# A hybrid S5, attention and MoE layer on one core: the opening's modulation, normalisation and S5 operator in another order

## The chip, the core and the metric

One core of a Trainium2 chip runs the whole kernel. The metric is the device time of one execution in microseconds. Three runs of the kernel before gave 2739.33 to 2745.31 us, with a median of 2741.16 us.

## The reference: what is computed

A layer over 1024 latent tokens of width 1024 and 256 context tokens, all in float32. Cut to what the opening touches:

```python
mod = silu(c) @ w_mod + b_mod              # for the latent and for the context vector
h   = layer_norm(x, g, b)                  # latent rows and context rows
u   = h * (1 + scale1) + shift1            # modulate
p   = u @ w_in                             # S5 input, q, k, v, gates
y   = S5_bidir(gelu input from p)          # 32 groups of 16 channels, 64 states
mix = W_o(sig(g_s) * W_s(GLU(y)) + sig(g_a) * W_a(attention))
h   = LN(alpha * h + gate1 * mix)
h   = LN(alpha * h + gate2 * MoE(modulate(h, shift2, scale2)))
```

The S5 recurrence is computed in blocks of 8 tokens: for each of 32 groups the kernel builds an operator within a block and the operators into and out of the state, from lam, b, c and d.

## The kernel before

The work up to about 300 us is called the opening here. It is written as Python generators, and `weave` takes one step of each in turn; `limit(gen, n)` takes at most n steps. That sets the order in which each engine gets its instructions, and each engine runs its own list strictly in that order. SyncE (SP) issues nearly all DMAs, also in order.

The parts, with their lines in the profile:

- `s5_consts`: the constants of the S5 blocks on DVE, with two loads of s5p.
- `mod_cols` (L1798): shift1 and scale1 as columns. Eight loads of w_mod (1 MB each, L1814, two buffers) feed 32 matmuls (L1827) with the two condition vectors `cs` stationary (2 columns) and 512 columns of w_mod moving, which leaves a row of 2x512; the trace shows two passes for each float32 matmul. ACT copies the row to SBUF (`mr`, L1831) and 16 transposes (L1834) turn it into columns of the PSUM tile `mod`. DVE adds the bias (`mc`, L1836) and makes the scale A and the shift B (L1843 to L1846).
- `ln_rows` (L1849), three groups: context, latent tiles 0 to 3, latent tiles 4 to 7. DVE takes BN_STATS (L78), a chain of small operations for the reciprocal root (L61 to L72) and normalises (L1860); the normalised latent rows are stored (`xhat_d`, L1862).
- `ln_cols` (L1866), the same three groups: PE transposes (L1874), ACT applies A and B (`f`, L1876) and takes the high part (`ch` or `uh`, L42), DVE the low part (`cl` or `ul`, L43). They are the moving and stationary sides of all projections, in which each product is three matmuls (L51 to L53).
- `s5_build` (L2107): for each of eight quarters of the groups `out(q)` makes `ca` on POOL (L2133 to L2135; the last two on DVE), `within(q)` copies `zb` (L2143), stores `ca` (`wout_d`, L2144), runs the matmuls `pm` and `pc` (L2151, L2154), evicts them (`qs`, L2157 to L2159) and stores eight pieces (`m_d`, L2162). `into(q)` makes `ba` on DVE (`cmul`, L1974 to L1981), transposes it (L2174), copies it to the one buffer `wi` on ACT (L2175) and stores it (`win_d`, L2177).
- `s_in(0)`, `s_in(1)` (L269): the projections of both halves of the S5 input. PE runs 24 matmuls for each step, ACT evicts `r` (L285); at the end of a half PE transposes it to `U` (L290, L295) and DVE copies U (L292, L296).
- `s5_state` (L355): loads the stored operator back (`wi`, L361), 16 groups `yp` for each half (L367), and their evictions `XS` on ACT and DVE (L370 to L372).
- `mod_rows` (L674): the six other parts of w_mod as rows. DVE multiplies and adds them (`macc`, L699, started by L701), eight pieces for each of eight chunks, with PE and DVE ending a chunk (L687, L688).
- After them `kv_rows`, `q_rows`, `gates`, `state_powers` (L379) and the scan.

In the kernel before, `opening` puts `out`, `within` and `into` between the normalisation and the columns, so part of the operator is built before the first projection.

Of the kernel before, what the change touches and what calls it, by code (L numbers as in the profile page):

```python
# [8 lines left out]
F32 = mybir.dt.float32  # L9
# [1488 lines left out]
def weave(*jobs):  # L1498

    jobs = [j for j in jobs if j is not None]  # L1500
    while jobs:
        for j in jobs[:]:
            if next(j, jobs) is jobs:
                jobs.remove(j)
# [293 lines left out]
def mod_cols(tc, a, K, xp, tmp):  # L1798

    nc = tc.nc  # L1800
    cst = K.cst
    sg = xp.tile([128, 16], F32, name="sg")
    cs = cst.tile([128, 8, 2], F32, name="cs")
    nc.scalar.activation(out=sg, in_=K.cols[:, 0:16], func=ACTF.Sigmoid)
    nc.vector.tensor_tensor(cs.rearrange("p k j -> p j k"), K.cols[:, 0:16].rearrange("p (j k) -> p j k", j=2),
                            sg.rearrange("p (j k) -> p j k", j=2), ALU.mult)
    K.cs = cs
    ws = []

    def load(n):  # L1810
        if n < 8:
            j, k = n // 2, n % 2 * 4
            w = K.wp.tile([128, 4, 512], F32, tag="raw", name="raw")
            nc.sync.dma_start(out=w, in_=a["w_mod"][k * 128:(k + 4) * 128, j * 512:(j + 1) * 512].rearrange("(k p) n -> p k n", p=128))  # L1814
            ws.append(w)

    load(0)
    load(1)
    yield
    tps = K.s5ps.tile([128, 512], F32, tag="mod", name="mod")  # L1820
    for j in range(4):
        p = K.mm.tile([128, 512], F32, tag="mm", name="mm")
        for h in range(2):
            w = ws.pop(0)
            for i in range(4):
                k = h * 4 + i
                nc.tensor.matmul(p[0:2, :], lhsT=cs[:, k, :], rhs=w[:, i, :], start=k == 0, stop=k == KT - 1)  # L1827
            load(2 * j + h + 2)
            yield
        mr = tmp.tile([128, 512], F32, tag="f", name="mr")[0:2]  # L1830
        nc.scalar.activation(out=mr, in_=p[0:2, :], func=ACTF.Copy)  # L1831
        for i in range(4):
            n = j * 4 + i
            nc.tensor.transpose(tps[:, 2 * n:2 * n + 2], mr[:, i * 128:(i + 1) * 128], K.ident[0:2, 0:2])  # L1834
    mc = xp.tile([128, 16, 2], F32, name="mc")
    nc.vector.tensor_tensor(mc, tps[:, 0:32].rearrange("p (a b) -> p a b", b=2),  # L1836
                            K.cols[:, 32:48].unsqueeze(2).to_broadcast([128, 16, 2]), ALU.add)
    K.A = cst.tile([128, 8, 2], F32, name="A")
    K.B = cst.tile([128, 8, 2], F32, name="B")
    g = K.cols[:, 16:24].unsqueeze(2).to_broadcast([128, 8, 2])  # L1840
    b = K.cols[:, 24:32].unsqueeze(2).to_broadcast([128, 8, 2])
    s1 = xp.tile([128, 8, 2], F32, name="s1")
    nc.vector.tensor_scalar(s1, mc[:, 8:16, :], 1.0, None, ALU.add)  # L1843
    nc.vector.tensor_tensor(K.A, s1, g, ALU.mult)
    nc.vector.tensor_tensor(K.B, s1, b, ALU.mult)
    nc.vector.tensor_tensor(K.B, K.B, mc[:, 0:8, :], ALU.add)  # L1846


def ln_rows(tc, a, K, xs, src, t0, n):  # L1849

    nc = tc.nc
    mv = K.sm.tile([128, 4, 2], F32, tag="mv", name="mv")
    r = K.sm.tile([128, 4], F32, tag="lir", name="lir")
    for i in range(n):
        ln_stats(nc, K.sm, xs[src, t0 + i], mv[:, i, :], "li")
        yield
    rsqrt(nc, K.sm, r[:, 0:n], mv[:, 0:n, 1], n, "li%d" % n)
    for i in range(n):
        x = xs[src, t0 + i]
        nc.vector.tensor_scalar(x, x, mv[:, i, 0:1], r[:, i:i + 1], ALU.subtract, ALU.mult)  # L1860
        if src == "x":
            nc.sync.dma_start(out=K.xhat_d[(t0 + i) * 128:(t0 + i + 1) * 128, :], in_=x)  # L1862
        yield
# [26 lines left out]
def opening(tc, a, K, pool, ls, fs, cs):  # L1890
# [21 lines left out]
    loads = [("x", 0, K.wp, "wlo"), ("x", 2, K.wp, "whi"), ("x", 4, K.wp, "wlo"), ("x", 6, hp, "x")]  # L1912
    load("ctx", 0, K.wp, "whi")
    next(s5)
    rows = [ln_rows(tc, a, K, xs, *g) for g in GROUPS]
    cols = [ln_cols(tc, a, K, tmp, xs, *g) for g in GROUPS]
    next(mods)
    weave(limit(s5, 31))
    next(mods)
    load(*loads.pop(0))  # L1920
    weave(s5, rows[0])
    next(mods)
    load(*loads.pop(0))
    outs, ins = s5_build(tc, a, K, sb)
    weave(limit(mods, 2))
    for x in loads:
        load(*x)
    weave(limit(mods, 2))
    next(outs)
    weave(limit(mods, 1))  # L1930
    w0, w1 = (load_raw(tc, K, a["w_in"][:, c * 256:(c + 1) * 256]) for c in range(2))
    weave(rows[1])
    weave(mods)
    weave(cols[0], rows[2])
    next(outs)
    weave(cols[1], limit(ins, 4))
    next(outs)
    w0 = load_w(tc, K, None, raw=w0)
    nc.sync.dma_start(out=K.rope, in_=a["rope"].rearrange("p (t j d) -> p t j d", t=8, j=3))
    weave(cols[2], limit(ins, 8))  # L1940
    next(outs)
    ls.close()
    K.rin = pool(cs, "rin", 1, side="right")
    w1 = load_w(tc, K, None, raw=w1)
# [18 lines left out]
def limit(gen, n):  # L1963
    for _ in range(n):
        if next(gen, gen) is gen:
            return
        yield
# [293 lines left out]
```

## Time and profile before

| | |
|---|---|
| runs | 2739.33 to 2745.31 us, median 2741.16 us |
| profiled execution | 2747.31 us, span 2745.2 us |
| PE busy | 2513.9 us (92%) |
| DVE busy | 2175.9 us (79%) |
| ACT busy | 1465.1 us (53%) |
| POOL busy | 275.4 us (10%) |
| granted clock of the core | 0.948 mean |

Busy shares over the whole span hide the stage at issue: the opening is a tenth of the span. It is read by stretches: the busy time and the granted clock between two events, the order of the events on each engine, and for each idle stretch the instruction that ended it.

### The profile page before, as it was taken

How to read it: one execution, taken by the hardware profiler on the slowest of the kernel's cores; microseconds unless marked ns; L12 is line 12 of the kernel's file. 1: busy time of each engine (PE TensorE's matmuls, PEld its weight loads, DVE VectorE, ACT ScalarE, POOL GpSimd, SP SyncE). 2: the span in 40 equal slices, each digit the busy share in tenths (PEclk: the TensorE clock that was granted, in tenths of full speed). 3: DMA queues.
4: the chain of work that ended last, by engine and by line, in shares of the span. 5: the costliest groups of instructions: out<-in, count | busy, mean ns of one | idle time of the engine just before them, and what ended most of it. 6: DMA issues, size and time to landing. Idle time of an engine off the chain costs nothing.

```text
span 2745.2 us, 41252 instructions
## 1 busy us (share of the span) xinstructions
PE 2513.9 (92%) x14030; PEld 2115.1 (77%) x14030; DVE 2175.9 (79%) x4203; ACT 1465.1 (53%) x2368; POOL 275.4 (10%) x173
## 2 busy tenths in 40 slices
PE   6799999888989886899999999999999999999990
PEld 1598887777778774788888878888988887888770
DVE  9635797337787757787887987988899899989995
ACT  0622112657766412565655655666666666666661
POOL 3300000000000004011010110111011111101103
PEclk8799999999999876899999999999999999999995
DMA  7434623544686783797987987998998999899974
GB/s 245 165 121 146 212 85 119 179 153 160 222 308 246 288 289 116 229 292 221 287 275 231 309 277 235 312 300 254 290 303 274 286 312 303 278 293 306 315 269 146
DMA packets 400934, 662.55 MB, mean 241 GB/s; under 512 B 36976, under 2 KB 203760, under 8 KB 393616
## 3 DMA queue, kind: packets, MB, share of 16 engines
q1 hardware_dynamic: 388416, 615.83, 67.2%
q0 software_dynamic: 11872, 42.47, 6.7%
q8 instruction: 112, 1.84, 0.3%
q10 hardware_dynamic: 432, 1.57, 0.2%
q14 instruction: 102, 0.84, 0.1%
HBM read 570.63 MB, written 89.15 MB: 240 GB/s over the span
## 4 chain that ended last, share of the span: by engine, by line
PE 46%; DVE 6%; issue 4%; DMA 2%; ACT 1%; POOL 0%; POOLq 0%; SPq 0%; DVEq 0%; ACTq 0%
PE uw L1360 14%; PE uw L1361 7%; PE dn L1307 6%; PE dn L1308 6%; PE dn L1310 5%; DVE wl L1494 2%; PE tp L1278 2%; PE up L1307 2%; PE up L1310 2%; PE up L1308 2%; DMA acc_d<-y,wi 1%; DVE oh L1198 1%; PE sl L1214 1%; ACT wh L1492 1%; PE up L1321 1%
## 5 line engine op out<-in xcount | busy, mean ns | idle before, releaser
L1494 DVE TENSOR_TENSOR wl<-raw,wh 128x1024 fp32r<-128x1024 f32 x768 | 921.6, 1220 | 162.7 <-ACT wh L1492 161.6
L1492 ACT ACTIVATE wh<-raw 128x1024 fp32r<-128x1024 f32 x768 | 789.5, 1052 | 243.5 <-PE dn L1310 88.7
L1360 PE MATMUL uw<-x,wh 128*128 128x320 f32 (+5 forms) x1920 | 580.5, 366 | 0.2 <-issue 0.2
L1361 PE MATMUL uw<-x,wl 128*128 128x192 f32 (+4 forms) x1920 | 501.2, 261 | 0.0
L1360 PEld LDWEIGHTS uw<-x,wh 128*128 128x128 f32 x1920 | 364.4, 190 | 23.8 <-issue 0.3
L1361 PEld LDWEIGHTS uw<-x,wl 128*128 128x128 f32 x1920 | 369.3, 192 | 0.5
L1307 PE MATMUL dn<-wh,a 128*128 128x512 f32 (+4 forms) x752 | 298.6, 397 | 0.0
L1308 PE MATMUL dn<-wl,a 128*128 128x512 f32 (+4 forms) x752 | 293.5, 390 | 0.0
L1310 PE MATMUL dn<-wh,a 128*128 128x512 f32 (+3 forms) x608 | 238.5, 392 | 0.6 <-DVE a L1287 0.6
L1307 PE MATMUL up<-wh,x 128*128 128x512 f32 x544 | 221.8, 408 | 0.0
L1443 POOL DMA_INDIRECT acc_d<-y,wi x47 | 120.7, 2568 | 959.2 <-DVE y L1441 815.9
L1310 PE MATMUL up<-wh,x 128*128 128x512 f32 x544 | 213.0, 392 | 0.0
L1308 PE MATMUL up<-wl,x 128*128 128x512 f32 x544 | 212.3, 390 | 0.0
L1372 ACT ACTIVATE t<-uw,bias 128x160 f32<-128x160 f32 (+5 forms) x240 | 98.6, 419 | 134.7 <-PE uw L1361 134.0
L1307 PEld LDWEIGHTS dn<-wh,a 128*128 128x128 f32 (+4 forms) x752 | 135.7, 180 | 37.8 <-issue 4.1
L1308 PEld LDWEIGHTS dn<-wl,a 128*128 128x128 f32 (+4 forms) x752 | 135.8, 181 | 33.8
L1310 PEld LDWEIGHTS dn<-wh,a 128*128 128x128 f32 (+3 forms) x608 | 112.8, 186 | 28.4 <-DVE a L1287 2.7
L1307 PEld LDWEIGHTS up<-wh,x 128*128 128x128 f32 x544 | 102.3, 188 | 27.4 <-issue 8.4
L1310 PEld LDWEIGHTS up<-wh,x 128*128 128x128 f32 x544 | 102.1, 188 | 22.4
L1308 PEld LDWEIGHTS up<-wl,x 128*128 128x128 f32 x544 | 102.4, 188 | 18.8
L51 PE MATMUL mm<-whi,uh 128*128 128x256 f32 x320 | 108.2, 338 | 4.7 <-DVE r L307 4.7
L52 PE MATMUL mm<-wlo,uh 128*128 128x256 f32 x320 | 107.5, 336 | 0.0
(528 smaller groups left out, 4939.8 us busy)
## 6 DMA issues: line engine op xcount, KB each, us to landing
raw<-w_gate_up SPq DMA_DIRECT2D x512, 512.0 KB
raw<-w_down SPq DMA_DIRECT2D x256, 512.0 KB
mw<-w_mod SPq DMA_DIRECT2D x64, 256.0 KB
raw<-w_in SPq DMA_DIRECT2D x13, 1024.0 KB
whi<-wo SPq DMA_DIRECT2D x10, 1024.0 KB
wlo<-wo SPq DMA_DIRECT2D x10, 1024.0 KB
raw<-w_mod SPq DMA_DIRECT2D x8, 1024.0 KB
gate_d<-gs SPq DMA_DIRECT2D x16, 512.0 KB
```

The lines of the kernel that those rows point to most:

```text
L51: nc.tensor.matmul(out, lhsT=lsel(lh, k), rhs=rsel(rh, k), start=start and k == 0, stop=False)
L52: nc.tensor.matmul(out, lhsT=lsel(lh, k), rhs=rsel(rl, k), start=False, stop=False)
L1278: nc.tensor.transpose(p[:, i * nb:(i + 1) * nb], rows(i), K.ident[0:nb, 0:nb])
L1307: nc.tensor.matmul(ps, lhsT=h, rhs=wh[:, k], start=st, stop=False)
L1308: nc.tensor.matmul(ps, lhsT=h, rhs=wl[:, k], start=False, stop=en and nb <= 64)
L1310: nc.tensor.matmul(ps, lhsT=X[:, k0 + k, lo:lo + nb], rhs=wh[:, k], start=False, stop=en)
L1360: nc.tensor.matmul(p[:, 0:2 * n], lhsT=wh[:, k, fs], rhs=self.x[:, k, 0:2 * n], start=k == 0, stop=False)
L1361: nc.tensor.matmul(p[:, 0:m], lhsT=wl[:, k, fs], rhs=self.x[:, k, 0:m], start=False, stop=k == KT - 1)
L1372: nc.scalar.activation(out=y[i], in_=self.uw[i][:, 1], func=ACTF.Identity, bias=self.bias[:, q * 8 + j0 + i:q * 8 + j0 + i + 1])
L1443: nc.gpsimd.indirect_dma_start(out=K.acc_d, out_offset=bass.IndirectOffsetOnAxis(ap=wi[0:nb], axis=0), in_=o[0:nb], in_offset=None, bounds ...
L1492: nc.scalar.activation(out=h, in_=r, func=ACTF.Copy)
L1494: nc.vector.tensor_tensor(l, r, h, ALU.subtract)
```

## The change

`mod_cols` makes w_mod the stationary side: for each block of 128 columns four matmuls (4 of the 8 blocks of rows, for one load) write two columns of `mod` directly, 128 matmuls in all. The sums over the two halves of the rows stand in two places of `mod`, and DVE adds them with one more operation. The rows `mr`, their copies and the transposes are gone.

`opening` issues the four loads of x right behind that of the context, ahead of the third load of w_mod. All rows are normalised and the modulation made, then the columns of the context and of the first latent half; only then are the first two pieces of w_in loaded and `s5_build` begun. Its remaining steps run beside the first projection and the start of the second. On SP the first store of `ca` (L2144), which stood right behind the last load of w_mod, now stands behind the eight stores of normalised rows, the two loads of w_in and that of the rotary table.

```diff
 def mod_cols(tc, a, K, xp, tmp):
     tps = K.s5ps.tile([128, 512], F32, tag="mod", name="mod")
     for j in range(4):
-        p = K.mm.tile([128, 512], F32, tag="mm", name="mm")
         for h in range(2):
             w = ws.pop(0)
             for i in range(4):
-                k = h * 4 + i
-                nc.tensor.matmul(p[0:2, :], lhsT=cs[:, k, :], rhs=w[:, i, :], start=k == 0, stop=k == KT - 1)
+                n = h * 16 + j * 4 + i
+                for k in range(4):
+                    nc.tensor.matmul(tps[:, 2 * n:2 * n + 2], lhsT=w[:, k, i * 128:(i + 1) * 128], rhs=cs[:, h * 4 + k, :], start=k == 0, stop=k == 3)
             load(2 * j + h + 2)
             yield
-        mr = tmp.tile([128, 512], F32, tag="f", name="mr")[0:2]
-        nc.scalar.activation(out=mr, in_=p[0:2, :], func=ACTF.Copy)
-        for i in range(4):
-            n = j * 4 + i
-            nc.tensor.transpose(tps[:, 2 * n:2 * n + 2], mr[:, i * 128:(i + 1) * 128], K.ident[0:2, 0:2])
     mc = xp.tile([128, 16, 2], F32, name="mc")
-    nc.vector.tensor_tensor(mc, tps[:, 0:32].rearrange("p (a b) -> p a b", b=2),
-                            K.cols[:, 32:48].unsqueeze(2).to_broadcast([128, 16, 2]), ALU.add)
+    half = lambda h: tps[:, h * 32:h * 32 + 32].rearrange("p (a b) -> p a b", b=2)
+    nc.vector.tensor_tensor(mc, half(0), K.cols[:, 32:48].unsqueeze(2).to_broadcast([128, 16, 2]), ALU.add)
+    nc.vector.tensor_tensor(mc, half(1), mc, ALU.add)
...
 def opening(tc, a, K, pool, ls, fs, cs):
     load("ctx", 0, K.wp, "whi")
     next(s5)
+    for x in loads:
+        load(*x)
     rows = [ln_rows(tc, a, K, xs, *g) for g in GROUPS]
     cols = [ln_cols(tc, a, K, tmp, xs, *g) for g in GROUPS]
-    next(mods)
-    weave(limit(s5, 31))
-    next(mods)
-    load(*loads.pop(0))
-    weave(s5, rows[0])
-    next(mods)
-    load(*loads.pop(0))
+    weave(limit(s5, 31), limit(mods, 2))
+    weave(s5, rows[0], limit(mods, 3))
+    weave(rows[1], mods)
+    weave(cols[0], rows[2])
+    weave(cols[1])
+    w0, w1 = (load_raw(tc, K, a["w_in"][:, c * 256:(c + 1) * 256]) for c in range(2))
     outs, ins = s5_build(tc, a, K, sb)
-    weave(limit(mods, 2))
-    for x in loads:
-        load(*x)
-    weave(limit(mods, 2))
-    next(outs)
-    weave(limit(mods, 1))
-    w0, w1 = (load_raw(tc, K, a["w_in"][:, c * 256:(c + 1) * 256]) for c in range(2))
-    weave(rows[1])
-    weave(mods)
-    weave(cols[0], rows[2])
-    next(outs)
-    weave(cols[1], limit(ins, 4))
-    next(outs)
     w0 = load_w(tc, K, None, raw=w0)
     nc.sync.dma_start(out=K.rope, in_=a["rope"].rearrange("p (t j d) -> p t j d", t=8, j=3))
-    weave(cols[2], limit(ins, 8))
-    next(outs)
+    weave(cols[2], limit(ins, 4))
     ls.close()
```

Lines behind L1950 keep their text and stand 17 lower in the changed kernel. Line numbers in this document are those of the kernel before.

The instruction lists show what the reordering does at three places. Behind `<-` stand the operands; `x16` counts equal instructions in a row. One matmul here is two passes in the trace.

TensorE at the start, before: `raw` is a load of w_mod, `pm` and `pc` belong to `within`, `tp<-ident,x` are the transposes of the columns.

```order
L1827 MATMUL mm<-raw,cs 2x512 x8
L2154 MATMUL pc<-bc,bb 16x16
L1834 MATMUL mod<-ident,mr 128x2 x4
L1827 MATMUL mm<-raw,cs 2x512 x8
...
L1827 MATMUL mm<-raw,cs 2x512 x4
L1874 MATMUL tp<-ident,x 128x128 x4
...
L1827 MATMUL mm<-raw,cs 2x512 x5
L1834 MATMUL mod<-ident,mr 128x2 x4
L1827 MATMUL mm<-raw,cs 2x512 x7
L1834 MATMUL mod<-ident,mr 128x2 x4
```

The same place after:

```order
L1827 MATMUL mod<-cs,raw 128x2 x32
L2137 MATMUL pc<-bc,bb 16x16 x8
L1827 MATMUL mod<-cs,raw 128x2 x16
L1870 MATMUL tp<-ident,x 128x128 x4
L1827 MATMUL mod<-cs,raw 128x2 x64
L2134 MATMUL pm<-ca,zb_704 48x128 x8
L2137 MATMUL pc<-bc,bb 16x16 x8
L1827 MATMUL mod<-cs,raw 128x2 x16
L1870 MATMUL tp<-ident,x 128x128 x4
```

Five of the eight loads of w_mod are now multiplied behind the first transposes of the normalised context, where before three were.

DVE around the modulation's end, before:

```order
L72 SCALAR_TENSOR_TENSOR lir<-li4t,li4y 128x4
L1860 TENSOR_SCALAR x<-x,mv,lir 128x1024 x4
L1836 TENSOR_TENSOR mc<-mod,cols 128x32
L1843 TENSOR_SCALAR s<-mc 128x16
L1844 TENSOR_TENSOR A<-s,cols 128x16
L1845 TENSOR_TENSOR B<-s,cols 128x16
L1846 TENSOR_TENSOR B<-B,mc 128x16
```

and after:

```order
L1856 TENSOR_SCALAR x<-x,mv,lir 128x1024 x2
L1832 TENSOR_TENSOR mc<-mod,cols 128x32
L1856 TENSOR_SCALAR x<-x,mv,lir 128x1024
L1833 TENSOR_TENSOR mc<-mod,mc 128x32
L1856 TENSOR_SCALAR x<-x,mv,lir 128x1024
L1839 TENSOR_SCALAR s_501<-mc 128x16
L1964 TENSOR_TENSOR ba<-cm_795,cm_796 128x512
L1840 TENSOR_TENSOR A<-s_501,cols 128x16
L1841 TENSOR_TENSOR B<-s_501,cols 128x16
L1957 TENSOR_TENSOR cm_947<-ip,bb 128x512
L1842 TENSOR_TENSOR B<-B,mc 128x16
```

`mc` stands ahead of two of the four normalisations, and between its parts stand pieces of `into`.

TensorE between the end of the second projection and the first rows of keys and values, before:

```order
L295 MATMUL tp<-ident,rc 128x32 x16
...
L367 MATMUL yp<-U,wi 128x160 x4
...
L367 MATMUL yp<-U,wi 128x160 x2
...
L367 MATMUL yp<-U,wi 128x160 x2
...
L53 MATMUL mm<-whi,ul 128x256
L367 MATMUL yp<-U,wi 128x160 x4
L687 MATMUL tp<-macc,ones 1x512
L290 MATMUL tp<-ident,r 128x128 x4
L367 MATMUL yp<-U,wi 128x160 x2
L51 MATMUL mm<-whi,ch 128x256 x2
```

and after, where `...` leaves out the projection's own matmuls:

```order
L2157 MATMUL tp<-ident,ba 128x128 x4
...
L290 MATMUL tp<-ident,r 128x128 x4
...
L53 MATMUL mm<-whi,ul 128x256
L290 MATMUL tp<-ident,r 128x128 x12
L295 MATMUL tp<-ident,rc 128x32 x16
L687 MATMUL tp<-macc,ones 1x512 x2
L367 MATMUL yp<-U,wi 128x160 x32
L51 MATMUL mm<-whi,ch 128x256 x2
L52 MATMUL mm<-wlo,ch 128x256
```

Nine `yp` groups and the first five transposes to `U` ran inside the second projection; now all 16 groups of the first half, and those transposes, stand behind its last step, with the operator's transposes (L2157) inside it.

## Rows read from the trace of the kernel before

**Rows 1.** Busy time by stage (start:end, length, busy us by engine, granted clock, DMA share, GB/s)
```profile
0.00:74.40 74.40, 45.74 (x148) 13.67 (x148) 68.49 (x220) 6.54 (x11) 25.10 (x26) 0.83 0.73 250
74.40:111.50 37.10, 22.93 (x130) 16.21 (x130) 26.12 (x34) 24.54 (x39) 15.85 (x12) 0.64 0.49 176
111.50:251.70 140.20, 139.29 (x756) 131.69 (x757) 61.39 (x96) 41.99 (x91) 5.50 (x4) 0.98 0.38 122
251.70:296.50 44.80, 39.66 (x261) 32.64 (x261) 36.89 (x57) 20.42 (x54) 0.00 (x0) 0.96 0.66 222
```

**Rows 2.** Timeline of DVE, 60 to 92 us (start us, us, line, names)
```profile
64.03 0.17 DVE L61 TENSOR_SCALAR li4v<-mv 128x4 f32<-128x4 f32 x1
...
70.45 0.16 DVE L72 SCALAR_TENSOR_TENSOR lir<-li4t,li4y 128x4 f32<-128x4 f32 x1
...
73.54 0.19 DVE L1836 TENSOR_TENSOR mc<-mod,cols 128x32 f32<-128x32 f32 x1
...
74.26 0.17 DVE L1846 TENSOR_TENSOR B<-B,mc 128x16 f32<-128x16 f32 x1
```

**Rows 3.** Timeline of POOL, 20 to 110 us
```profile
62.89 1.26 POOL L2135 TENSOR_TENSOR ca<-cg 128x512 f32<-128x512 f32 x1 [20.88 <-DMA wout_d<-ca]
```

**Rows 4.** Lines by form, 0 to 150 us (count | busy us, mean ns | idle before)
```profile
L1827 PE MATMUL mm<-raw,cs 128*2 128x512 f32 x64 | 32.6, 662 | 11.6 <-DMA raw<-w_mod 11.6
...
L1876 ACT ACTIVATE f<-tp,B,A 128x512 f32<-128x512 f32 x16 | 12.4, 776 | 13.7 <-PE tp L1874 10.2 <-DVE cl L43 2.0 <-DVE ul L43 1.3
...
L42 ACT ACTIVATE uh<-f 128x512 fp32r<-128x512 f32 x16 | 9.8, 622 | 0.1
...
L1860 DVE TENSOR_SCALAR x<-x,mv,lir 128x1024 f32<-128x1024 f32 x10 | 7.5, 807 | 0.1
...
L1975 DVE TENSOR_TENSOR cm<-ip,bb 128x512 f32<-128x512 f32 x7 | 5.8, 828 | 0.0
```

**Rows 5.** Timeline of PE, 43 to 80 us
```profile
45.81 0.90 PE L1874 MATMUL tp<-ident,x 128*128 128x128 f32 x3 [0.25 <-DVE x L1860]
...
56.03 0.41 PE L1834 MATMUL mod<-ident,mr 2*128 2x2 f32 x4
```

**Rows 6.** Timeline of PE, 108 to 116 us, start of the first projection
```profile
111.53 0.58 PE L52 MATMUL mm<-wlo,ch 128*128 128x256 f32 x1 [0.21 <-DVE wlo L43]
111.91 0.42 PE L53 MATMUL mm<-whi,cl 128*128 128x256 f32 x1
112.12 0.42 PE L51 MATMUL mm<-whi,ch 128*128 128x256 f32 x1
```

**Rows 7.** Timeline of DVE, 60 to 115 us, from the context's columns on
```profile
76.13 1.18 DVE L43 TENSOR_TENSOR cl<-f,ch 128x256 fp32r<-128x256 f32 x2 [1.26 <-ACT ch L42]
...
81.28 1.19 DVE L43 TENSOR_TENSOR cl<-f,ch 128x256 fp32r<-128x256 f32 x2 [1.25 <-ACT ch L42]
...
109.19 2.29 DVE L43 TENSOR_TENSOR wlo<-raw,whi 128x2048 fp32r<-128x2048 f32 x1
```

**Rows 8.** Waits, 0 to 345 us (us in total, times, longest us)
```profile
ACT wi L2175 <- DMA win_d<-wi: 12.9, 5, 4.9
```

**Rows 9.** Lines by form of PE, 112 to 150 us
```profile
L2151 PE MATMUL pm<-ca,zb 128*48 128x128 f32 x48 | 7.5, 281 | 0.0
...
L2174 PE MATMUL tp<-ident,ba 128*128 128x128 f32 x36 | 5.7, 282 | 0.0
```

**Rows 10.** Lines by form of PE, 180 to 296.5 us
```profile
L367 PE MATMUL yp<-U,wi 128*128 128x160 f32 x128 | 22.4, 309 | 1.4 <-DVE XS L372 1.1
...
L290 PE MATMUL tp<-ident,r 128*128 128x128 f32 x32 | 4.9, 283 | 0.0
```

**Rows 11.** Lines by form of DVE, 251.7 to 296.5 us
```profile
L372 DVE COPY XS<-yp 64x320 f32<-64x320 f32 x23 | 15.0, 708 | 1.6 <-ACT XS L371 1.1
L699 DVE SCALAR_TENSOR_TENSOR macc<-mw,cs,macc 128x512 f32<-128x512 f32 x14 | 10.5, 749 | 0.3
```

**Rows 12.** Timeline of DVE, 249 to 300 us
```profile
296.55 0.48 DVE L701 TENSOR_SCALAR macc<-mw,cs 128x512 f32<-128x512 f32 x1
```

## The prediction

> **What bounds the kernel now.** I read the busy time by stage first [rows 1]. Up to 74.4 us DVE is the engine without pause (68.5 of 74.4 us), TensorE has 45.7. From 74.4 to 111.5 nobody is full: TensorE 22.9 of 37.1 at a granted clock of 0.64, DVE 26.1, ACT 24.5. There the chain of transposes, ACT, DVE and back sets the pace, and the operator's build stands in the same lists. From 111.5 to 251.7 TensorE is full (139.3 of 140.2): the two projections of the S5 input. From 251.7 to 296.5 it is nearly full (39.7 of 44.8) with DVE at 36.9. So a step taken out of the second stage and put into the third costs there what TensorE spends on it, and no more, as long as its waits don't come along.
>
> Then the events. On DVE `mc` starts at 73.54 behind four normalisations, and B is done at 74.43 [rows 2]. In the ten microseconds ahead, thirteen small DVE operations of 0.16 us, from 64.03 to 70.45 [rows 2], take 6.6 us, while six POOL operations run from 62.89 on [rows 3]. I read the stretch as DVE held up by POOL.
>
> **The change, part by part.** The sum is made against the profiled execution, 2747.3 us (span 2745.2), which lies 6.1 above the median of the runs, 2741.2; the difference is then taken from the median.
>
> First, **B**. Ahead of `mc` DVE loses two normalisations (0.81 each), two `cm` and a `ba` (0.83 each) [rows 4]: 4.1 us, with five small copies left out. The second burst on POOL waits for a store of `ca`; that store now stands behind the normalised rows and two loads of w_in on SP, so the burst comes later and 13 x 0.16 = 2.1 us stand for 6.6: another 4.5, of which I take 4.2, as a few of them would be slow anyway. `mc` could start at 73.5 - 8.3 = 65.2. From there to B stand `mc`, a second half of it, two normalisations, the `ba`, a `cm` and four small ones: 4.2 us. B: 69.4, 5.0 earlier. Ends: 74.4 if POOL hinders as before, 66 if the copies count too.
>
> TensorE must not be later. The context's transposes end at 46.7 [rows 5], as their rows were normalised at the same place; BN_STATS of later tiles stand ahead of them now, and these fill what POOL leaves. Behind them come five loads of w_mod, 32 passes each, with 128 columns stationary and two moving. The nearest row is the old transposes of the modulation, also 128 stationary columns by two: four in 0.41 us [rows 5], 0.10 each. Five loads: 16 us, plus about 2.4 for a `within`, gives 65.1, level with DVE. Twice that price is the far end, for the projection's passes with 128 stationary columns start 0.21 apart at half clock [rows 6] (more moving columns, so an upper end): 33.6 us and B at 87. I take 0.10, whose form is the same. In sum the old matmuls kept TensorE busy for 32.6 us [rows 4], the new ones do so for 25.6 at 0.10, so its gain from the new form is small; the way over ACT and back is what is gone.
>
> The Trainium skill (TensorE: Matmul & The Clock Gate, LDWEIGHTS) says that the load of the stationary side takes its number of columns over 1.2 ns, 107 ns for 128 columns, whatever moves. It speaks against this change, which loads 128 columns for two; by that figure, an estimate, five loads are 17.1 us and B, and with it the end, come about 1 us later than I take it.
>
> The four loads of x now pass the third load of w_mod on SP. That one lands up to 17 us later (4 MB at the stage's mean of 250 GB/s [rows 1]), but TensorE needs it and the fourth only around 46 us, when the normalised context comes. I cost this at nothing; if that cover fails, L1827 waits for DMA, and the price is at most the 11.6 us of such waits now [rows 4].
>
> Second, **the columns, B to the first matmul with `wlo`**, 37.1 us now. The context's: four pairs, `cl` at 76.13 and two pairs on at 81.28 [rows 7], 2.6 each, 10.4 for all. The latent half's eight: ACT needs 0.78 + 0.62 = 1.4 each [rows 4], 11.2, and the split of w_in adds a part of its 2.3 [rows 7], say 1. Together 22.6, first matmul at 92.0, 19.5 earlier. What falls away are the waits of `into` and `within` among them: five waits of `wi` for its store, 12.9 us, longest 4.9 [rows 8], and `zb`, `cm`, `ba` and `wlo` in DVE's line. Ends: 21.6 (the split hidden) and 32 us (a latent tile as slow as a pair of the context's).
>
> Third, **from there to the end of the second projection**. The first projection takes in what was done earlier: two `within`, 32 of 48 passes of `pm` at 7.5 us [rows 9], 5.0; two `into`, 16 of 36 at 5.7, 2.5; small `pc` passes 0.5: 8.0. Out of it go the nine `yp` groups, 36 of 128 passes at 22.4 us [rows 10], 6.3, and the transposes to U, 16 of 32 at 4.9 [rows 10], 2.2 with their small ones left out: 8.5. So 140.2 stays 139.7 and the end moves from 251.7 to 231.7, 20.0 earlier. The `within` and `into` have about 130 us for what takes TensorE 20, so their DMA waits are hidden by 24 matmuls to a step, unless they stand head of line; bounds 0 to +6.5, half the waits of `wi`.
>
> Fourth, **what is given back**. Behind the projection DVE holds the bound: 36.9 us until the start of the sixth chunk of `macc` at 296.55 [rows 12], 44.9 after the end. Now it gets nine more evictions XS at 0.71, eleven more `macc` at 0.75 [rows 11], five copies to U (0.7 each), two adds and a start: 6.4 + 8.2 + 3.5 + 1.9 = 20.0, so 56.9 us. TensorE gets 39.7 + 8.5 = 48.2, no longer the bound. I take 57.5; the lower end is 56.9, the upper 64.8 with the 7.9 us in which DVE was idle now. The sixth chunk starts at 289.2 instead of 296.5.
>
> From this chunk on the order on every engine is the same as before, so the difference stays: -7.3. That is 2740.0 for a profiled execution, and 2733.9 against the median. The terms, shortly: B -5.0, columns -14.5, projections -0.5, the tail +12.6.
>
> **The rivals.** *The waits move along.* `wi` has one buffer, each store must land before the next copy, and TensorE's transposes and ACT's `r` stand behind it in line. If half of the 12.9 us [rows 8] comes up in the first projection, 6.5 of 7.3 are gone: within 2 us of the median, 2740. For it: all eight `into` now run there. Against: with over 100 us, a store needs its 3 to 5 us once per several steps. Chance 0.22.
>
> *DVE stays as slow ahead of B.* If the POOL burst stays or the loads of x come late, B stays at 74, the columns alone remain (-14.5, -0.5, +12.6 = -2.4): 2739. That is the case in which the reordering of rows and modulation doesn't do what it says. Chance 0.08.
>
> *Slower: the stationary loads.* If a pass costs 0.21, each load is 6.7 us, the buffers chain them, and B comes at 87, 18 later than forecast: -7.3 + 18 = +11, 2752. TensorE runs this at half clock (0.64 in the next stage [rows 1]), and with two columns moving there is nothing to hide a load of 128 behind. It decides from a pass of 0.15 on: 46.7 + 2.4 + 160 x 0.15 = 73.1, B at 77. Against it: the old transposes of this form at 0.10. Chance 0.14.
>
> *More than forecast.* If the clock, with fewer gaps among the columns, comes back before the first projection, the 5 us of it at half clock cost half (-2.5), and the columns run 2 to 5 shorter: -13, 2728, or more where B is at 66. Chance 0.16.
>
> **How the numbers follow.** Forecast (-6 to -11): 0.40. A measurement of this kernel tells about 0.2%, 5.5 us, from no change. Faster by that: 0.40 + 0.16 = 0.56. Within: 0.22 + 0.08 = 0.30. Slower: 0.14. The range goes from 2721 (-20, the third stage's whole gain kept) to 2747 (+6, a pass at 0.18), which leaves out the larger part of the slower case and little of the others.
>
> **What would show it.** B at 69, first `wlo` matmul at 92, end of the second projection at 232, sixth chunk at 289, all in the timeline. Wrong, if DMA or `wi` ends TensorE's waits between 92 and 232; if a pass of L1827 starts over 0.15 us after the one before; if a stretch behind the second projection has DVE idle for more than some 8 us; or if the difference at the sixth chunk doesn't equal that at the end.

## The result and the profile after

The changed kernel takes 2775.64 us (median of 4 runs, 2772.19 to 2777.88) against 2740.89 for the kernel before beside it: a ratio of 1.0112, 95% interval 1.0098 to 1.0126. It is slower, by 35 us; forecast were 7.3 us less, and the time lies outside the range. The profiled execution took 2776.04 us, span 2774.1.

Line numbers of the changed kernel are 4 lower than those of before up to `ln_cols` (L1870 for L1874) and 17 lower behind (L2160 for L2177); the runs further down have numbers of their own, so go by the names there. First the busy time by stage, to be held against [rows 1], with the stages cut at the same events (columns as there):

```profile
0.00:85.40 85.40, 61.01 (x308) 59.63 (x308) 57.95 (x216) 4.20 (x7) 16.96 (x20) 1.00 0.60 219
85.40:108.50 23.10, 12.85 (x62) 8.12 (x62) 14.63 (x21) 20.06 (x30) 11.81 (x8) 0.81 0.63 207
108.50:250.10 141.60, 137.52 (x770) 132.29 (x770) 59.96 (x88) 39.75 (x80) 19.38 (x15) 0.95 0.29 88
250.10:321.50 71.40, 53.52 (x334) 44.34 (x334) 55.54 (x85) 26.36 (x73) 0.00 (x0) 0.93 0.63 213
```

In the first stage TensorE's busy time rose from 45.7 to 61.0 us and DVE's fell from 68.5 to 58.0: the bound has changed sides. The second stage is as short as forecast. The last one holds the surprise: neither DVE (55.5 of 71.4 us) nor TensorE (53.5) fills it.

By the prediction's own four terms, each the distance between the same two events. The columns before and after date B and the end of the projection by the start of their last instruction, the forecast by its end; that shifts a boundary by 0.2 to 0.4 us and leaves the measured changes as they are.

| stage | before | forecast | after | change forecast | change measured |
|---|---|---|---|---|---|
| start to B | 74.3 | 69.4 | 85.3 | -5.0 | +11.0 |
| B to the first `wlo` matmul | 37.3 | 22.6 | 23.3 | -14.5 | -14.0 |
| to the end of the second projection | 139.8 | 139.7 | 141.6 | -0.5 | +1.8 |
| to the sixth chunk of `macc` | 45.3 | 57.5 | 71.5 | +12.6 | +26.2 |
| sum, the sixth chunk | 296.55 | 289.2 | 321.56 | -7.3 | +25.0 |

**Ahead of B.** The timeline of TensorE, 26 to 84 us, after (`raw` is the stationary side now):

```profile
29.06 6.99 PE L1827 MATMUL mod<-cs,raw 128*128 128x2 f32 x32 [3.79 <-DMA raw<-w_mod]
42.57 1.41 PE L1870 MATMUL tp<-ident,x 128*128 128x128 f32 x4 [6.52 <-DVE x L1856]
43.78 27.31 PE L1827 MATMUL mod<-cs,raw 128*128 128x2 f32 x128
71.01 3.65 PE L2134 MATMUL pm<-ca,zb 128*48 128x128 f32 x16
74.59 0.61 PE L2137 MATMUL pc<-bc,bb 128*16 128x16 f32 x16
75.13 6.99 PE L1827 MATMUL mod<-cs,raw 128*128 128x2 f32 x32
```

128 passes in 27.31 us are 0.213 each. TensorE stands idle for 6.5 us before the context's transposes, which wait for DVE, and then has five loads of w_mod in front of it. The timeline of DVE, 57 to 86 us, shows who pays:

```profile
57.51 0.15 DVE L72 SCALAR_TENSOR_TENSOR lir<-li4t,li4y 128x4 f32<-128x4 f32 x1
57.58 0.21 DVE L2126 COPY zb<-bb 64x128 f32<-64x128 f32 x1
57.72 1.52 DVE L1856 TENSOR_SCALAR x<-x,mv,lir 128x1024 f32<-128x1024 f32 x2
82.15 0.19 DVE L1832 TENSOR_TENSOR mc<-mod,cols 128x32 f32<-128x32 f32 x1 [22.92 <-PE mod L1827]
...
85.25 0.17 DVE L1842 TENSOR_TENSOR B<-B,mc 128x16 f32<-128x16 f32 x1
```

DVE is through at 59.2, earlier than forecast (65.2), as the stretched small operations of [rows 2] are gone: five of the thirteen took 0.95 to 1.12 us there, beside POOL's work from 62.9 to 70.0, and here, with POOL idle from 40.2 to 96.3, they take 0.14 to 0.16. Then DVE waits 22.92 us for TensorE.

**Behind the second projection.** SP's own timeline, 225 to 262 us (when a DMA was issued), then TensorE's:

```profile
238.98 0.33 SPq L2160 DMA_DIRECT2D win_d<-wi  x1
239.40 2.46 SPq L696 DMA_DIRECT2D mw<-w_mod  x3
245.18 0.33 SPq L2160 DMA_DIRECT2D win_d<-wi  x1
245.60 5.66 SPq L696 DMA_DIRECT2D mw<-w_mod  x2
251.42 0.33 SPq L2160 DMA_DIRECT2D win_d<-wi  x1
252.87 0.33 SPq L361 DMA_DIRECT2D wi<-win_d  x1
```

```profile
260.15 4.76 PE L367 MATMUL yp<-U,wi 128*128 128x160 f32 x20 [3.22 <-DMA wi<-win_d]
```

The stores of the operator come once in 6.2 us, as its steps are woven into the projection. Each stands in SP's line and holds up all behind it; the last leaves at 251.42, and only then is the operator loaded back. The first `yp` runs at 260.15; before, nine groups were done by 251.3. The waits in SP's queue, 108 to 321.5 us (total, times, longest), name the instruction:

```profile
SPq L2160 <- ACT wi L2158: 50.3, 9, 15.7
SPq L696 <- DVE macc L699: 26.5, 20, 4.9
```

Before, the same wait (L2177) came to 19.9 us from 108 to 300 us, and to 29.7 from the start on, as part of the operator was built earlier there.

### The profile page after: what moved, and what is told of

Read it like the earlier page. It is cut to its first block, busy times and chain, and to the rows that moved or that the text cites. A ratio compares the mean times of both kernels' runs of the same rounds, so it can differ in the third digit from the quotient of the medians.

```text
span 2774.1 us, 41611 instructions
## 1 busy us (share of the span) xinstructions
PE 2535.3 (91%) x14206; PEld 2167.2 (78%) x14206; DVE 2171.9 (78%) x4204; ACT 1462.5 (53%) x2364; POOL 273.4 (10%) x173
## 5 line engine op out<-in xcount | busy, mean ns | idle before, releaser
L1492 ACT ACTIVATE wh<-raw 128x1024 fp32r<-128x1024 f32 x768 | 789.6, 1052 | 244.1 <-PE dn L1310 88.7
L53 PE MATMUL mm<-whi,ul 128*128 128x256 f32 x320 | 108.3, 339 | 2.3 <-DVE ul L43 2.3
```

The source lines that it names most:

```text
L53: nc.tensor.matmul(out, lhsT=lsel(ll, k), rhs=rsel(rh, k), start=False, stop=last)
L1492: nc.scalar.activation(out=h, in_=r, func=ACTF.Copy)
```

## The experiments

To add up what a kernel does, one event more is used: the first L480 (transposes of `zrow`), at 583.9 us before. It follows TensorE's whole work of the opening, and the order up to there differs little between the kernels. Busy and idle time of TensorE up to that event make up its place by definition; what the runs test is whether a distance at that event is still there at the end. Before, then after (columns as in [rows 1]):

```profile
0.00:583.90 583.90, 517.53 (x2787) 423.25 (x2788) 378.59 (x703) 187.75 (x316) 46.45 (x42) 0.94 0.47 155
```

```profile
0.00:610.20 610.20, 535.13 (x2963) 473.10 (x2963) 374.36 (x704) 184.58 (x312) 48.15 (x42) 0.97 0.45 148
```

So of 26.3 us, 17.6 are more busy time of TensorE and 8.7 more idle time (66.4 to 75.1). Busy time is not the number of matmuls alone: the modulation's take 20.7 us more (55.1, for 32.6 and 1.8 of transposes), while `pm` and `pc`, as many as before, take 9.3 less (23.4 for 32.7), most of them now beside the projections at a granted clock of 0.95, where many stood in stages at 0.83 and 0.64 [rows 1]. In the spans the difference is 28.9. All runs below are read by this account. It was formed after the first eight of them (theory C in the later expectations); theory D, on the clock, came after e12.

| run | B | first `wlo` | busy | idle | first L480 | ratio (95%) |
|---|---|---|---|---|---|---|
| before | 74.3 | 111.5 | 517.5 | 66.4 | 583.9 | 1 |
| after | 85.3 | 108.5 | 535.1 | 75.1 | 610.2 | 1.0112 (1.0098 to 1.0126) |
| e1_order_only | 78.0 | 100.9 | 517.4 | 69.2 | 586.6 | 1.0004 (0.9994 to 1.0015) |
| e2_cols_only | 69.4 | 109.5 | 529.5 | 54.3 | 583.8 | 1.0011 (0.9997 to 1.0026) |
| e3_store_act | 85.3 | 108.6 | 535.7 | 59.7 | 595.4 | 1.0033 (1.0023 to 1.0043) |
| e4_build_early | 83.1 | 127.5 | 528.0 | 72.2 | 600.2 | 1.0079 (1.0063 to 1.0096) |
| e5_order_store | 77.1 | 100.1 | 512.8 | 72.0 | 584.8 | 1.0013 (1.0002 to 1.0024) |
| e6_mod_first | 78.4 | 103.7 | 539.3 | 67.6 | 606.9 | 1.0119 (1.0102 to 1.0136) |
| e7_before_store | 73.8 | 107.1 | 520.4 | 69.0 | 589.4 | 1.0022 (1.0009 to 1.0036) |
| e8_mw_pool | 85.4 | 108.7 | 542.9 | 88.7 | 631.6 | 1.0186 (1.0168 to 1.0203) |
| e9_fill_new | 71.1 | 96.6 | 527.1 | 49.4 | 576.5 | 0.9963 (0.9948 to 0.9978) |
| e10_fill_old | 74.1 | 101.6 | 509.7 | 64.4 | 574.1 | 0.9979 (0.9966 to 0.9992) |
| e11_both_forms | 119.7 | 159.2 | 582.0 | 49.3 | 631.3 | 1.0178 (1.0144 to 1.0212) |
| e12_first_store | 78.7 | 103.9 | 534.9 | 52.0 | 586.9 | 1.0017 (1.0005 to 1.0028) |
| e13_wide | 72.7 | 95.8 | 533.0 | 65.9 | 598.9 | 1.0057 (1.0038 to 1.0076) |
| e14_wide_store | 79.0 | 104.2 | 531.4 | 52.5 | 583.9 | 1.0002 (0.9987 to 1.0018) |
| e15_wide_fill | 73.9 | 100.0 | 519.2 | 55.4 | 574.6 | 0.9991 (0.9975 to 1.0006) |
| e16_wide16 | 83.1 | 106.5 | 539.3 | 72.3 | 611.6 | one run, 2776.86 us |

**e1_order_only and e2_cols_only** take the change apart: e1 is the changed kernel with the old `mod_cols`, e2 the kernel before with the new one.

```diff
 # e1: changed kernel, old mod_cols
-                    nc.tensor.matmul(tps[:, 2 * n:2 * n + 2], lhsT=w[:, k, i * 128:(i + 1) * 128], rhs=cs[:, h * 4 + k, :], ...)
+                nc.tensor.matmul(p[0:2, :], lhsT=cs[:, k, :], rhs=w[:, i, :], ...)
 # e2: the kernel before with the opposite edit
```

> The changed kernel with the old modulation columns (the two condition vectors stationary, 512 columns of w_mod moving, rows copied by ACT and transposed); the new order stays. Theory A, two separate losses (128 stationary columns at 0.21 us a pass, and a tail behind the second projection that is long because the operator is stored late): B at 68 to 73 us instead of 85, first wlo matmul at 91 to 96, the tail from the end of the second projection to the sixth macc chunk still 68 to 72 us, time 2758 to 2764. Theory B, one loss (the long tail only follows from the late B): tail back to 57 or 58, time 2742 to 2748.

> The kernel before with the new modulation columns alone (w_mod stationary); the old order stays. Theory A: eight loads at 32 passes of 0.21 us are 54.5 us of TensorE instead of 33, B 5 to 14 us later than the 74.4 of before, the tail as before at 44 to 46 us, time 2746 to 2755. Theory B: the same late B also lengthens the tail by some 13 us, time 2758 to 2768. If TensorE's idle time ahead of B holds the new passes, no change: 2741.

Neither half alone moves the time by more than can be told, and both together cost 1.12%. The expectations hold in part: e1's time is that of theory B, but its tail of 64.9 us fits neither theory; e2's time is that of its third case, and its B came 5 us earlier than before. In e2 TensorE works 12 us more and idles 12 us less: the dear passes fill time in which it waited anyway (28.5 us idle ahead of B before, 9.8 in e2). In the changed kernel that time is still there ahead of the context's transposes (7.5, 3.3, 3.8 and 6.5 us), but the passes of five loads stand behind them, where TensorE works without a pause from 42.6 to 82.1. In e1, B is 3.7 us later than before even with the old form, since DVE still waits for TensorE, and its last small operations are stretched again, beside POOL's work from 74.3 on (timeline of DVE in e1):

```profile
74.21 1.44 DVE L2130 COPY zb<-bb 64x128 f32<-64x128 f32 x2 [8.45 <-PE pm L2138]
75.68 0.19 DVE L1836 TENSOR_TENSOR mc<-mod,cols 128x32 f32<-128x32 f32 x1
75.91 0.87 DVE L1843 TENSOR_SCALAR s<-mc 128x16 f32<-128x16 f32 x1
76.81 1.02 DVE L1844 TENSOR_TENSOR A<-s,cols 128x16 f32<-128x16 f32 x1
...
77.95 1.22 DVE L1846 TENSOR_TENSOR B<-B,mc 128x16 f32<-128x16 f32 x1
```

So in the new order the first term fails with the old form too, though by less; no run has a new pass at the forecast price. In e1 the sixth chunk of `macc` starts 10.8 us later than before (307.31), and the end of the span is 1.0 later: the event at which the prediction closed its sum doesn't carry to the end.

**e3_store_act** puts the stores of the operator on ACT's queue. **e8_mw_pool** instead moves the loads of `mod_rows` (`mw`) away from SP, to POOL's queue.

```diff
 # e3
-nc.sync.dma_start(out=K.win_d[b][:, c0:c0 + 512], ...)
+nc.scalar.dma_start(out=K.win_d[b][:, c0:c0 + 512], ...)
 # e8
-nc.sync.dma_start(out=w, in_=a["w_mod"][k * 128:(k + 1) * 128, 2 * D ...
+nc.gpsimd.dma_start(out=w, in_=a["w_mod"][k * 128:(k + 1) * 128, 2 * D ...
```

> The changed kernel with one thing other: the sixteen stores of win_d are issued from ACT's queue, right behind the copy they store, instead of SP's, so that the loads of mw for the macc chunks no longer stand behind them on SP. Theory A with SP's queue as the cause: macc fills DVE's idle time during the projections again, tail 55 to 60 instead of 71 us, B unchanged at 85, time 2760 to 2766. If the tail is long for another reason (the late copy to U, the load of wi behind the last store): tail 66 to 72, time 2771 to 2778.

> The changed kernel with the 64 loads of mw (for the macc chunks) on POOL's queue; the stores of win_d and the loads of wi stay on SP. If the loads of mw behind the stores are what lengthens the tail: macc runs through the projections again, tail 55 to 62 us instead of 71, 10 to 18 us of the 31 us loss regained. If it is the load of wi behind the last store: tail 66 to 72, less than 5 us regained.

e3 regains 14.7 us in the spans (2759.4 for 2774.1) and 15.4 of TensorE's idle time, with B and the columns unchanged to 0.1 us. The `yp` groups run again inside the second projection (timeline of TensorE in e3):

```profile
254.83 0.70 PE L367 MATMUL yp<-U,wi 128*128 128x160 f32 x4
...
261.12 1.79 PE L367 MATMUL yp<-U,wi 128*128 128x160 f32 x12
```

In the changed kernel the queue behind the stores is shown to be worth that much. e8 leaves the stores where they were and is slower still; its `wi` also comes back late (first `yp` at 258.65), but 64 loads on POOL's queue change more than the one thing, so it tells only that taking `mw` out of the line is no mend.

**e5_order_store and e7_before_store** make e3's edit with the old form of the columns (in e1) and in the kernel before.

> The changed kernel with the old modulation columns and with the stores of win_d issued from ACT's queue: only the new order is left, without the queue behind SP. If the two losses add (B late by the stationary side, SP's queue held by the stores) and both are gone here: B at 74 to 79 us, the tail from the end of the second projection to the sixth macc chunk 50 to 57 us, 8 to 16 us faster than the kernel before. If the order alone already carries the queue's cost hidden elsewhere (it was within 1 us of the kernel before): within 4 us of before.

> The kernel before with the stores of win_d on ACT's queue, a control. If the stores hold up SP's queue only where the operator is built beside the projections: within 3 us of the kernel before. If ACT's queue is better anywhere, 5 to 10 us faster, and what the other run gained by it is no sign of the changed order.

There the stores gain nothing (1.0013 and 1.0022, both a little slower), and the 8 to 16 us expected of e5 did not come. The length of the waits on SP does not tell the two cases apart: in e1 the same stores wait 46.4 us, nearly as long as the 50.3 in the changed kernel. With the stores moved, TensorE's idle time between 240 and 330 us falls from 18.5 to 8.7 us in the changed kernel and stays at 12.0 in e1. Why the line is a bound with the new form and not with the old, no run shows.

**e4_build_early** begins `s5_build` ahead of the first latent half's columns again and puts steps of `within` and `into` back among the columns.

```diff
+    next(outs)
+    next(outs)
-    weave(cols[1])
+    weave(cols[1], limit(ins, 4))
+    next(outs)
-    weave(cols[2], limit(ins, 4))
+    weave(cols[2], limit(ins, 8))
+    next(outs)
```

> The changed kernel with the operator's steps back where the kernel before has them (two within and out ahead of the latent columns, four steps of into with those of the first latent half, eight with the second), the new modulation and the rows first. Theory A: B at 80 to 87, the columns 32 to 37 us again, first wlo matmul at 115 to 122, but the tail back to 45 to 50 us; time 2747 to 2757. Theory B: the tail stays at 65 to 72 with B that late, time 2770 to 2780.

The distance from the second projection to the sixth chunk goes back to 46.9 us, and the columns cost 44.4 (37.3 before): what the change took out of one place returns in the other, and by the ratios only 9 of 31 us are regained.

**e6_mod_first and e12_first_store.** e6 issues the loads of w_mod ahead of those of x and takes two steps of `mods` first, so that TensorE multiplies one load more before the context's transposes; e12 is e6 with e3's stores.

```diff
-    for x in loads:
-        load(*x)
-    weave(limit(s5, 31), limit(mods, 2))
+    next(mods)
+    next(mods)
+    for x in loads:
+        load(*x)
+    weave(limit(s5, 31))
```

> The changed kernel with the loads of x moved behind the third and fourth load of w_mod, so that TensorE multiplies four loads instead of three ahead of the context's transposes. If B is late because TensorE stands idle from 21 to 43 us and then has five loads at 7 us each in line: B at 76 to 80 instead of 85 us, first wlo matmul at 99 to 104, and 5 to 8 us of the 31 us loss against the kernel before regained. If B is bound elsewhere: B stays at 84 to 86, no more than 2 us regained.

> The changed kernel with both mends together: four loads of w_mod ahead of the context's transposes (the loads of x behind the third and fourth) and the stores of win_d on ACT's queue. The first alone left the loss against the kernel before at 30 us, the second alone at 11. If the first fails only because SP's queue eats what it brings: 3 to 7 us slower than the kernel before. If it brings nothing: 10 to 14 us slower.

B comes 6.8 us earlier in e6, and at the end almost nothing of it is left (3.3 us at the first L480, none in the ratio): the line on SP keeps its pace, and the distance to the sixth chunk grows from 71.5 to 74.1. With the stores out of the line e12 comes within 6 us of the kernel before (2751.94 against 2746.15). e3's mend alone left 9 us by the ratios and e6's alone regained nothing: by the place of the first L480 the earlier B pays only once the line on SP is clear (8.5 us from e3 to e12, for 3.3 from the changed kernel to e6). By the ratios e3 and e12 overlap.

**e11_both_forms** is the kernel before with four added passes of the new form behind each old matmul (128 matmuls, their results unused).

> The kernel before with the new form's 128 matmuls added beside the old ones, into an unused part of the same PSUM tile: 256 passes more, 54.5 us of TensorE at 0.21 each, nothing else. Theory C: some 20 of the 28.5 us in which TensorE is idle ahead of B take a part of it, the rest goes to the end: 28 to 38 us slower than the kernel before, idle time ahead of B down to 8 to 12 us. If DVE set the opening's pace: 10 us slower or less. If a pass costs less where the old form stands between: below 20.

TensorE's work grows by 64.5 us, its idle time shrinks by 17.1, and the end is 47 later. That work of TensorE ends up on the path is seen. The idle time ahead of B fell as expected (28.5 to 8.4); the size was missed because TensorE's work grew by 10 us more than the 54.5 put in. The old matmuls, unchanged, were slowed by the company (lines by form of e11, 0 to 120 us):

```profile
L1827 PE MATMUL mm<-raw,cs 128*2 128x512 f32 x64 | 52.0, 908 | 7.6 <-DMA raw<-w_mod 7.6
L1830 PE MATMUL mod<-cs,raw 128*128 128x2 f32 x256 | 51.7, 324 | 0.0
```

They took 52.0 us for the 32.6 of [rows 4]: 0.90 a pass up to 73 us and again from 98 us on, and 0.48 between, behind runs of `pm` and `pc`, where the new passes fall to 0.12 as well. So the added passes cost more than their own time.

**e9_fill_new and e10_fill_old** are the kernel before with two moves only: the split of w_in stands ahead of the columns of the first latent half, and no steps of `into` stand among these; e9 has the new form of the modulation, e10 the old.

```diff
+    w0 = load_w(tc, K, None, raw=w0)
-    weave(cols[1], limit(ins, 4))
+    weave(cols[1])
     next(outs)
-    w0 = load_w(tc, K, None, raw=w0)
```

> The kernel before with the new modulation columns, and with two moves: the split of the first piece of w_in stands ahead of the first latent half's columns, and no step of into among these columns (the four steps run later). Theory C, by the busy and idle time of TensorE up to its first transposition of z (583.9 us in the kernel before, of these 66 idle): TensorE is what ends this stretch, so only its busy and idle time count. B at 69 as with the new columns alone, first wlo matmul at 90 to 95 instead of 109, idle time among the columns 8 to 12 instead of 18 us, and 6 to 12 us faster than the kernel before. If DVE's tail behind the projections counts: within 3 us of before, or slower.

> The same two moves (split of w_in earlier, no into among the first latent columns) with the old modulation columns. Theory C: B at 74 as before, first wlo matmul at 95 to 100 instead of 111.5, TensorE's busy time unchanged, 4 to 10 us faster than the kernel before. If the steps of into only move on and stall TensorE later: within 3 us.

These are the two that beat both kernels, e9 with 2736.33 us against 2746.15 beside it, e10 with 2741.04. The first projection starts 15 and 10 us earlier than before. The account of e9:

```profile
0.00:576.50 576.50, 527.07 (x2963) 468.01 (x2963) 377.35 (x704) 183.23 (x312) 49.84 (x42) 0.95 0.48 157
```

TensorE idles 17 us less and works 9.5 more. So the columns' own gain can be had, if the build stays mostly where it was and the passes stand where TensorE waits. Between e9 and e10 the intervals overlap, so nothing is shown for the new form itself. In e10 the gain at the first L480 is not one of waiting: of 9.8 us, 7.8 are less busy time with the same matmuls, where none was expected, and only 2.0 less idle time. In both runs the first projection starts 1.6 us later than expected.

**e13_wide, e14_wide_store, e15_wide_fill, e16_wide16** ask why a pass takes 0.213. One thing had stood out in e2. Its timeline of TensorE:

```profile
42.21 3.88 PE L1827 MATMUL mod<-cs,raw 128*128 128x2 f32 x32
46.14 1.41 PE L1870 MATMUL tp<-ident,x 128*128 128x128 f32 x4
47.34 20.48 PE L1827 MATMUL mod<-cs,raw 128*128 128x2 f32 x96
```

and the busy time of these stretches:

```profile
42.20:46.00 3.80, 3.80 (x33) 3.79 (x32) 3.80 (x12) 0.00 (x0) 0.00 (x0) 0.95 0.02 4
47.40:57.00 9.60, 9.60 (x47) 9.60 (x47) 9.47 (x29) 0.00 (x0) 0.00 (x0) 0.50 0.98 358
```

The same pass takes 0.121 us at a granted clock of 0.95 and 0.213 at 0.50. The runs let each pass move 64 (or 16) columns, the two repeated: e13 and e16 in the changed kernel, e14 in e12, e15 in e9. The sums then stand in another order in `mod`, and DVE adds them with three small operations more; the cut shows the matmul only.

```diff
-nc.tensor.matmul(tps[:, 2 * n:2 * n + 2], lhsT=..., rhs=cs[:, h * 4 + k, :], ...)
+nc.tensor.matmul(tps[:, 2 * n:2 * n + 64].rearrange("p (r j) -> p r j", j=2), lhsT=..., rhs=cs[:, h * 4 + k, :].unsqueeze(1).to_broadcast([128, 32, 2]), ...)
```

> The changed kernel, but each pass of the modulation's columns moves 64 columns (the two, 32 times over) where it moved 2; the stationary side and the number of passes stay. Theory D (clock): the passes took 0.213 us because TensorE stood at its lower level all the time up to B, although the record shows 1.00 there; in the run with the columns alone 32 of them took 3.88 us, 0.121 each, right after other work had brought the level up. With more columns moving the level comes up during the passes as it did with the old ones of 512 columns: 0.12 to 0.15 a pass, more work in less time, 160 passes behind the context's transposes in 19 to 24 us instead of 34, B at 69 to 75 instead of 85, end of the second projection at 235 to 242. The queue is not mended, so a part is lost again behind the projection: ratio 1.004 to 1.011. Rival (the load itself costs 0.21 at any level, or a pass can only get longer with more columns): 0.21 to 0.27 a pass, B at 85 to 95, ratio 1.011 to 1.016.

> The changed kernel with the first loads of the modulation ahead of the rows, the stores of the operator on ACT's queue (together 1.0017 before) and 64 columns moving. Theory D: B at 66 to 71 instead of 78.7, end of the second projection 6 to 12 earlier than 253.6, and as the queue is mended most of it stays: ratio 0.9965 to 1.0000. Rival (load itself): B at 78 or later, ratio 1.001 to 1.006.

> The kernel before with the new columns, the split of w_in ahead of the latent half and no operator's steps among the columns (0.9963 before), and 64 columns moving. Theory D: 0.12 to 0.15 a pass, B at 65 to 70 instead of 71.1, where DVE or the load of w_mod sets it next, TensorE busy 15 to 22 us less up to B and idle more by nearly as much less the gain in B: ratio 0.9945 to 0.9965. Rival (load itself): B at 71 or later, 0.996 to 1.000.

> As e13_wide with 16 columns moving. Theory D leaves open whether 16 are enough to bring the level up: either 0.12 to 0.15 a pass as there, or 0.21 as with 2. Rival (load itself): 0.21 to 0.23.

TensorE's timeline in e13:

```profile
44.25 13.76 PE L1827 MATMUL mod<-cs,raw 128*128 128x64 f32 x64
57.94 3.65 PE L2136 MATMUL pm<-ca,zb 128*48 128x128 f32 x16
61.52 0.61 PE L2139 MATMUL pc<-bc,bb 128*16 128x16 f32 x16
62.06 3.79 PE L1827 MATMUL mod<-cs,raw 128*128 128x64 f32 x32
65.78 1.51 PE L2136 MATMUL pm<-ca,zb 128*48 128x128 f32 x12
67.22 3.79 PE L1827 MATMUL mod<-cs,raw 128*128 128x64 f32 x32
```

0.215 a pass up to 58, 0.118 from 62 on, and `pm` goes with it, 0.228 and 0.126. The rival (such a load costs 0.21 at any level) falls; of theory D the half that it is TensorE's level stands, the other half falls: with 64 columns moving the passes of 7.8 to 21.6, 29.0 to 42.9 and 44.3 to 58.0 are as slow as with two, and the fast ones came behind `pm` and `pc`. The 64 columns cost nothing, either. In e16, with 16 columns, 128 passes took 27.33 us (0.214 each) and the last 32, behind `pm` and `pc`, 4.60 (0.144). In e14 all passes stay slow (32 in 7.09 us) and B is where e12 had it; e15 has both paces, and its time can't be told from the kernel before. e13's B at 72.7 has a second cause besides the level: 64 passes, not 32, stand ahead of the context's transposes there (29.02 to 42.9). By these rows, an estimate, 32 passes fewer behind the transposes are 6.8 us and 64 faster ones 6.1, so the level is about half of what B gained. Its earlier B, 12.5 us, is 11.3 at the first L480 and 14.7 in the medians, as a ratio 1.0057 for 1.0112.

## Why the prediction was wrong

- **B (forecast -5.0, measured +11.0).** The step that failed is "Five loads: 16 us ... I take 0.10, whose form is the same". A pass measured 0.213, and 160 of them took 34.3 us, not 16. The row of the old transposes [rows 5] was no equal: its stationary side has 2 partitions, not 128, and it ran at a granted clock of 1.00, the upper of TensorE's two levels (2.4 GHz). Even at that level the new form takes 0.12 (e2, e13), by which the five loads are 19 us, an estimate. The rival "the stationary loads" had the price (0.21), the reason (the lower level, 1.2 GHz) and B (87 for 85.3); it got 0.14. The row that the prediction called the far end [rows 6] was the right one.
- **The clock.** The rest of the price is TensorE's level: 0.121 a pass at a granted clock of 0.95 and 0.213 at 0.50 in e2. The Trainium skill (TensorE: Matmul & The Clock Gate, LDWEIGHTS) puts the load of the stationary side at its number of columns over 1.2 ns, which makes 107 ns for 128 columns. The rows at the upper level come near that (0.118 to 0.121), the passes of the changed kernel (0.213) don't, and the measurement decides. The prediction used the figure only as a small correction to the wrong row.
- **DVE's part of B** was right in kind: it was through at 59.2, and the burst on POOL did come later, at 96.3. It bought nothing, as TensorE had become the later one; e1 shows the same with the old form.
- **The columns (-14.5, measured -14.0) and the projections (-0.5, measured +1.8)** came out. In the second, TensorE idles 3.2 us more than before and works 1.4 less, for 0 and 0.5 in the sum, so it came out in size only.
- **The tail (+12.6, measured +26.2).** DVE's work was counted well, 55.5 us for 56.9; TensorE's came to 53.5 for 48.2. What failed is "a store needs its 3 to 5 us once per several steps", which priced the stores of `wi` by their own wait and against ACT alone. They stand in SP's line ahead of the loads of the operator and of `mw`. The wait for the store itself was rightly dismissed (ACT's `wi` waits 0.8 us for it now, 12.9 before [rows 8]); what is queued behind the stores waits (e3: 15.4 us of idle time).
- **"From this chunk on the order on every engine is the same as before, so the difference stays".** In the changed kernel +25.0 became +28.9 in the span; in e1 +10.8 became +1.0. The chunk is DVE's event, and TensorE has work of `kv_rows`, `q_rows` and `gates` to run meanwhile. The distances at TensorE's first L480 carry better: the spans differ from before by the same to within 5.2 us in all sixteen runs. That is still 5 us of play, as large as the effects of e2 and e7.
- **The sum of it.** The rival's own sum, +11, was too small, as it was made with the forecast's tail. Form and order cost together what neither costs alone: the form added 12 to 18 us of busy time, the order put most of its passes behind the idle time that could hide them, and with the new form the line on SP ate what came early. Without the last, and with one load more ahead of the transposes, the ratio is 1.0017 (e12).

Left open: what brings TensorE up from its lower level. It came up behind runs of `pm` and `pc` (e2, e11, e13, e16) and not in 64 to 128 passes of the new form, whether 2 or 64 columns moved. But such a run is not enough: in the changed kernel 32 passes behind 16 `pm` and 16 `pc` (71.0 to 75.2 us) still took 6.99 us, 0.218 each, and in e2 the level fell again with TensorE busy almost without a pause. The 8.7 us of additional idle time in the changed kernel were only split as far as e3 and e6 do it.

## What to carry to other kernels

Price a matmul form by a row with the same number of stationary rows and columns, and at the lower level of the clock if the work around it doesn't hold the upper one. When a step is moved beside other work, list its DMAs in each queue and ask what stands behind them, not who waits for them. Close the sum on the engine that ends the stretch, as its work plus its idle time: added work is free where that engine waited, and a reordering that puts the work behind the waiting takes that cover away.

## What the runs showed of the hardware that was not expected

The granted clock of the record doesn't show the level at the start. In the changed kernel it reads 1.00 up to 85.4 us, while all 128 passes from 43.78 on took 0.213 us, the duration that e2's record has at 0.50; e13 has both paces at a recorded 1.00:

```profile
7.80:57.90 50.10, 43.20 (x212) 42.41 (x212) 49.59 (x181) 0.35 (x2) 16.01 (x14) 1.00 0.74 272
58.00:61.90 3.90, 3.90 (x31) 3.41 (x31) 3.84 (x8) 0.28 (x1) 0.18 (x1) 1.00 0.58 153
62.10:71.00 8.90, 8.90 (x78) 8.58 (x78) 5.31 (x4) 0.59 (x2) 7.24 (x6) 1.00 1.02 401
```

Until the record has a first change, the level is better read from the distance of equal instructions. A pass with 128 stationary columns costs the same with 2 and with 64 columns moving (0.213 and 0.215).
